# Sixty-four-row scores and state products widened to all 128 rows of the array in a hybrid-mixer trunk

## The chip, the cores and the metric

The kernel runs on one core of one Trainium2 chip. The metric is the device time of one execution in microseconds, from the first instruction to the last. Three executions of the kernel before stand beside one profiled execution.

## The reference

Two layers work on 256 context tokens and 256 latent tokens of width 1024. Each layer normalises, projects the input once, runs four mixers in parallel on the columns (A a gated recurrence, B an mLSTM, C grouped-query attention, D latent attention), merges them with gates, projects out, and adds a squared-ReLU MLP. Cut to what the change touches:

```python
# C: 8 query heads of 64 on 2 key heads; D: scores of 128 plain and 64 rotary columns
s = jnp.einsum('bqhgd,bmhd->bhgqm', qi, k) * scale
p = jax.nn.softmax(s, axis=-1)
return jnp.einsum('bhgqm,bmhd->bqhgd', p, v)
# B: q, k of 64 columns; cmat is the 64 x 128 state that the context left
s = jnp.einsum('bhtk,bhsk->bhts', qc, kc) * jnp.exp(dmat - m_t[..., None])
num = w_inter[..., None] * jnp.einsum('bhtk,bhkv->bhtv', qc, cmat) + jnp.einsum('bhts,bhsv->bhtv', s, vc)
```

In layer 0 the mixers answer for context and latent tokens, in layer 1 for the latent tokens alone.

## The kernel before, in words

Features or keys stand on the 128 partitions, so a product contracts over the rows of TensorE's array. Large products are made from numbers split into a high and a low part, in three passes (L193 to L195 and L215 to L217 for the input, gate, output and MLP weights, L164 to L166 for the branch weights). Weights come by DMA as `raw` tiles on SP's queue; ScalarE writes the high part `whi` (L136) and VectorE the low part `wlo` (L137).

The order of the work is written by hand: the string `ORDER` lists for each layer the steps of the mixers (`b` is one head of B on one side, `c` one pair of heads of C, `d` one head of D) and of the merges (`M0` to `M3`). A scheduler then lays the instructions of each engine out in one fixed order, in which the large products stand between the small ones of the mixers. Each engine takes its instructions in that order.

Scores of 64 columns (C, and the rotary part of D) are made by `score64`. `split_pair` puts a head's 64 high query rows on one half of the partitions and its low rows on the other half, in one tile `T`. `dup_key` writes the high key and the low key each on both halves. The first pass (L961) multiplies all 128 rows of `T` with the doubled high key. The second pass (L962) takes only the 64 high query rows and the 64 rows of the low key beside them. A softmax follows: maximum (L977, VectorE), exponential (L980, ScalarE), reciprocal and scaling (L982, L983, VectorE), and, two softmaxes later, the transposes of the probabilities on TensorE (L233), copied out by ScalarE (L989).

In B the scores of a head contract over 64 rows (L874). L879 broadcasts the running maximum with 100 rows. For each direction `d` the numerator sums up to three products into one PSUM tile (L907): probabilities `E` times values (128 rows, `bv` in the profile), and for the latents the scaled queries `qw` times the context state `C` (64 rows, those of the head). These are plain f32 operands, and each such product stands in the trace as two MATMULs. `qw` is written by ScalarE (L896) and VectorE (L897) on the head's 64 rows.

L400 is a product of the adaLN modulation that fills gaps, with 32 columns of the array. Scratch tiles of 2 KB a partition come from the pool `w2`, which has ten of them.

Of the kernel before, what the change touches and what calls it, by code (L numbers as in the profile page):

```python
# [23 lines left out]
# order of the mixers' steps and of the merges, by layer  # L24
# [16 lines left out]
class Trunk:  # L41
# [58 lines left out]
    def wide(self):  # L100
        """a pair of weight tiles out of the mixers' room."""
        t = self.t("w8", [128, 2, 1024], F32R)
        return t[:, 0, :], t[:, 1, :]

    def _prep(self):
        nc = self.nc
# [7 lines left out]
        n = 0  # L114
# [16 lines left out]
        with ExitStack() as st:  # L131
            # not in the way of a norm that the products wait for
            for ins in self.first[:2]:
                st.enter_context(self.tc.issue_after(ins))
            self.first = self.first[2:]
            nc.scalar.activation(out=hi[:, 0:n], in_=raw[:, 0:n], func=AF.Copy)  # L136
            nc.vector.tensor_tensor(out=lo[:, 0:n], in0=raw[:, 0:n], in1=hi[:, 0:n].bitcast(F32), op=ALU.subtract)  # L137
        self.ready[i] = (hi, lo)

    def get(self, key):  # L140
        if self.specs[self.next_use][2]:
            self.ada_sum()
        i = self.next_use
        assert self.specs[i][0] == key, (self.specs[i][0], key)
        # none ahead where a norm waits for the engines
        look = 0 if key[0] == "out" and key[2:] == (3, 1) or key[0] == "f2" and key[2:] == (3, 3, 1) else self.look
        while self.next_prep < min(i + 1 + look, len(self.specs)):
            self._prep()
        self.next_use += 1
        w = self.ready.pop(i)  # L150
        if self.specs[i][2]:
            # the modulation of a later phase, one chunk at a time
            n = self.next_use
            if n < len(self.specs) and self.specs[n][0][0] == "ada":
                self.ada_chunk(self.specs[n][0])
        return w

# [1 line left out]
    def mm3(self, out, pairs):  # L159
        """pairs: list of ((lhs_hi, lhs_lo), (rhs_hi, rhs_lo))."""  # L160
# [7 lines left out]
    def fm(self, W, t0, t1, nk=KT, c0=0, stride=128, act=None):  # L168
        """feature-major product: out[c, tok] for 128 columns of chunk W."""
# [7 lines left out]
    def fm2(self, key, t0, t1, act=None):  # L177
        """feature-major products for the 256 columns of two chunks, half of the rows in each."""
# [18 lines left out]
    def tm(self, key, i0):  # L197
        """token-major product: out[tok, 256 columns]; yields (first tile, psum [128, 2, 256])."""
# [9 lines left out]
    def tm_k(self, o, W, k, i):  # L208
# [4 lines left out]
        # one start per bank: it clears the written bits of both tiles  # L213
# [11 lines left out]
    def plan_cols(self, key, w, c0, halves=(0, 1), dest=None, fill=True):  # L225
        """256 columns of w, half of the rows at a time."""
# [9 lines left out]
    def setup(self):  # L236
# [22 lines left out]
        # puts a sum over the partitions in its row  # L259
# [13 lines left out]
        # conditioning columns  # L273
# [7 lines left out]
        # lower bounds of the second layer: softmax over the two layers  # L281
# [6 lines left out]
        # residual stream, feature-major; the first norm's statistics come from the token-major tiles  # L288
# [24 lines left out]
    def setup_late(self):  # L313
        """tables that only the mixers need."""
# [13 lines left out]
        # rotary tables with the key / query gains folded in  # L328
# [20 lines left out]
    def ada_vec(self, key):  # L349
        """the same on VectorE: running sums over the feature tiles, then one sum over the partitions."""  # L350
# [39 lines left out]
    def ada_chunk(self, key):  # L390
# [7 lines left out]
        for q in range(4):  # L398
            # one start per quadrant: it clears the written bits of both halves
# [33 lines left out]
    def stat(self, t0, k):  # L433
        """adds feature tile k of the tokens from t0 to the running sum of squares."""
# [25 lines left out]
    def warm_sqrt(self, src):  # L460
        """loads the square root's table ahead of its use."""
        d = self.sm([128, 1], "warm")
        self.nc.scalar.activation(out=d, in_=src, func=AF.Sqrt, scale=0.0)

    def rsqrt(self, ms, scale, out=None):
        """(scale * ms + eps) ** -0.5 on a small [128, n] operand."""
# [28 lines left out]
    # weights that follow the modulation of each feature tile  # L495
# [47 lines left out]
    def start(self):  # L543
        nc = self.nc
        W, out, at = {}, {}, {}
        for c in range(KT + 1):
# [7 lines left out]
            # the products, one feature tile behind  # L554
# [25 lines left out]
    def mixer_a(self, l, pre):  # L580
# [4 lines left out]
        if l:  # L585
            # the context first, while the latents are still being normalised
# [31 lines left out]
    def a_head(self, l, j, F, K, Q, KKs, q, V, O, q0, i0):  # L618
        nc = self.nc
        nt = 4 - i0  # L620
        # Q[0]: backward, Q[1]: forward
# [11 lines left out]
        for lev in range(8):  # L633
# [10 lines left out]
            else:  # L644
                # blocks of 128: across the two tiles of a side
# [8 lines left out]
            # grow the blocks  # L654
# [17 lines left out]
        # state left by the context  # L672
# [25 lines left out]
    def head_stats(self, O, out, i0):  # L698
        """mean squares of the heads of 128."""
# [6 lines left out]
    def readout(self, l, O, r, key, silu, gcol, i0, name):  # L706
        nc = self.nc
        for i in range(i0, 4):
            # half, for the gate is 1 + tanh
# [33 lines left out]
    def conv(self, l, qk, mt, ps, q0, scale):  # L743
        """three taps along the tokens of each side, then SiLU."""
# [15 lines left out]
    def mixer_b(self, l):  # L760
# [9 lines left out]
        for i2, ps in self.tm(("kv", l, 0), 0):  # L770
            # columns i_fwd, f_fwd, i_bwd, f_bwd to row groups 0, 64, 32, 96
# [8 lines left out]
        # log sigmoid of the forget gates on rows 0..3 (forward) and 32..35 (backward)  # L780
# [17 lines left out]
        # running maxima; the latents start from the maximum the context left  # L798
# [12 lines left out]
        # rows 64..: m = b + M  # L811
        nc.vector.tensor_tensor(out=UM[64:64 + R], in0=bc[0:R], in1=M[0:R], op=ALU.add)
        # -M as two parts on rows 0.. and 64.., for the broadcast over the partitions
# [4 lines left out]
        # broadcast of the end values over the partitions  # L818
# [7 lines left out]
        # u and m with tokens on partitions  # L826
# [10 lines left out]
        # keys, queries, values  # L837
# [8 lines left out]
        # context state  # L846
# [21 lines left out]
        for (sd, t0) in sides:  # L868
            for h in range(HEADS):
# [6 lines left out]
                for d in range(2):  # L876
# [5 lines left out]
                    full = d          # the key tile that meets both query tiles  # L882
# [11 lines left out]
                    if sd:  # L894
                        qw = self.t("w2", [128, 512])[:, 0:256]
                        nc.scalar.activation(out=qw[p0:p0 + 64], in_=pM[p0:p0 + 64, 0:256], func=AF.Exp, bias=ME[p0:p0 + 64, 1, row:row + 1])  # L896
                        nc.vector.tensor_tensor(out=qw[p0:p0 + 64], in0=qw[p0:p0 + 64], in1=qT[mt][p0:p0 + 64, t0:t0 + 256], op=ALU.mult)  # L897
                    pn = self.pm()
                    for tt in range(2):
# [4 lines left out]
                        if sd:  # L904
                            srcs.append((qw[p0:p0 + 64, tt * 128:(tt + 1) * 128], C[p0:p0 + 64, d, mt, :]))
# [16 lines left out]
    def rope(self, out, src, cos, sin, nh, eng):  # L922
        """out = src * cos + swap(src) * sin on [128, nh, 64]; cos, sin [128, 64]."""
# [10 lines left out]
    def dup_key(self, ps, p0, name):  # L934
        """hi and lo of the 64 rows of ps at p0, each on both halves of the partitions."""
# [10 lines left out]
    def split_pair(self, ps, q0, scale=1.0):  # L946
        """two heads of 64 rows: for each, hi on its own rows and lo on the other half."""
        nc = self.nc
        out = []
        for p0 in (0, 64):  # L950
# [5 lines left out]
            out.append((T, a))  # L956
        return out

    def score64(self, o, T, c, key, ns, start, stop):
        T, a = T  # L960
        self.nc.tensor.matmul(o, T[:, c], key[0][:, 0:ns], start=start, stop=False)  # L961
        self.nc.tensor.matmul(o, T[a, c], key[1][a, 0:ns], start=False, stop=stop)  # L962
# [10 lines left out]
    def softmax_t(self, ps, ns, PTdst):  # L973
        """softmax over the free axis of ps [128, ns]; probabilities transposed into PTdst [128, ns/128, 128]."""
# [19 lines left out]
    def run_later(self, depth=0):  # L994
        """second halves of the softmaxes, and what follows them, up to so many behind the first halves."""
# [114 lines left out]
    def mixer_d(self, l):  # L1110
# [11 lines left out]
        # latent keys and values  # L1122
# [11 lines left out]
        # rotary key, shared by the heads  # L1134
# [10 lines left out]
        # latent queries  # L1145
# [80 lines left out]
    def merge(self, l, r, Y, q0, js=range(4)):  # L1226
# [4 lines left out]
        for j in js:  # L1231
# [6 lines left out]
            if r == 3:  # L1238
                # the first weights of the MLP
# [66 lines left out]
    def ff(self, l, q0):  # L1306
        nc = self.nc
        # both halves of the hidden features in one tile where the latents alone need it
# [5 lines left out]
        for c in range(4):  # L1314
            if c == 0:
                # the context first, while the latents are still being normalised
# [17 lines left out]
            for p in range(4):  # L1334
                if l == 0 and c == 3 and p == 2:
                    self.ahead = [[self.get(("ai", 1, j, half)) for half in range(2)] for j in range(2)]
                if l == 0 and c == 3 and p == 3:
                    # the context first, so that its norm runs under the latents' products
# [33 lines left out]
    def run(self):  # L1372
# [81 lines left out]
        # final norm on the token-major output  # L1454
# [14 lines left out]
    def to_out(self, k):  # L1469
        """feature tile k of the latents, times the last gain, to the token-major output."""  # L1470
# [22 lines left out]
def layout(inputs):  # L1493
# [9 lines left out]
    # constants of the shapes  # L1503
# [32 lines left out]
```

## Time and profile before

| | |
|---|---|
| three executions | 1874.95, 1878.17 and 1880.63 us, median 1878.17 us |
| span of the profiled execution | 1878.2 us |
| TensorE busy | 1836.9 us (98% of the span), 11414 MATMULs |
| VectorE, ScalarE, GpSimd busy | 1135.8, 836.6 and 118.7 us |
| DMA | 235.26 MB, 125 GB/s on average |

The profiled execution is the span: nothing lies around it. In the timeline of TensorE the first number is the start in microseconds and the second the duration of the row; matmuls overlap, so what one occupies is the distance from its start to the next start, and not its duration. A form such as 64\*128 gives the rows and the columns of the array that the instruction uses.

### The profile page before, as it was taken

What the parts mean: (1) busy time and instruction counts of PE and PEld (TensorE: products, weight loads), DVE (VectorE), ACT (ScalarE), POOL (GpSimd) and SP (SyncE); (2) the same over time, 40 slices, a digit from 0 to 9 for tenths busy, and PEclk for the clock granted to TensorE, in tenths of its full rate; (3) what the DMA queues carried; (4) which work ended last, traced back from release to release, by engine and by line L of the source; (5) the groups of instructions that cost most, each with busy time, mean ns of one, the idle gap of its engine ahead of it and who ended that gap; (6) DMA issues with size and microseconds to landing.
All of it is one profiled execution on the core that took longest, in us unless ns stands there. A gap on an engine that the chain in (4) does not pass through costs nothing.

```text
span 1878.2 us, 28645 instructions
## 1 busy us (share of the span) xinstructions
PE 1836.9 (98%) x11414; PEld 1558.4 (83%) x11414; DVE 1135.8 (60%) x1983; ACT 836.6 (45%) x1487; POOL 118.7 (6%) x123
## 2 busy tenths in 40 slices
PE   7999999999999999999999999999999999999998
PEld 5788877799667778898777888988889969889998
DVE  5566654527654443566766665588574856575665
ACT  4343433434663333443333334344454664555555
POOL 0000000000001111111010000000000001101110
PEclk9999999999999999999999999999999999999999
DMA  9533353333112233314565665222334514454654
GB/s 284 178 91 108 117 147 123 90 107 90 46 34 68 68 124 101 113 46 146 168 190 177 185 187 158 79 68 68 89 114 141 161 52 135 144 161 145 185 185 136
DMA packets 222343, 235.26 MB, mean 125 GB/s; under 512 B 8320, under 2 KB 209408, under 8 KB 221952
## 3 DMA queue, kind: packets, MB, share of 16 engines
q1 hardware_dynamic: 222208, 233.42, 41.6%
q8 instruction: 90, 1.47, 0.3%
q14 instruction: 45, 0.37, 0.1%
HBM read 229.20 MB, written 4.19 MB: 124 GB/s over the span
## 4 chain that ended last, share of the span: by engine, by line
PE 86%; DVE 5%; DMA 4%; ACT 2%; issue 2%; SPq 0%; POOL 0%; ACTq 0%; DVEq 0%; POOLq 0%
PE pd L193 13%; PE pd L195 13%; PE pd L194 13%; PE pd L215 5%; PE pd L216 4%; PE pd L217 4%; PE pd L164 4%; PE pd L165 4%; PE pd L166 4%; DMA raw<-in_w_ada_dram 4%; PE pm L233 3%; PE pm L642 2%; DVE wlo L137 2%; PE pm L907 2%; PE pm L962 1%
## 5 line engine op out<-in xcount | busy, mean ns | idle before, releaser
L137 DVE TENSOR_TENSOR wlo<-raw,whi 128x1024 fp32r<-128x1024 f32 x305 | 385.9, 1265 | 301.4 <-ACT whi L136 299.8
L136 ACT ACTIVATE whi<-raw 128x1024 fp32r<-128x1024 f32 x305 | 322.0, 1057 | 402.6 <-PE pd L194 163.5
L195 PE MATMUL pd<-HH,wlo 128*128 128x256 f32 (+1 forms) x1104 | 373.2, 338 | 9.4 <-DVE wlo L137 9.4
L193 PE MATMUL pd<-HH,whi 128*128 128x256 f32 (+1 forms) x1104 | 374.0, 339 | 0.2 <-ACT whi L136 0.2
L194 PE MATMUL pd<-HL,whi 128*128 128x256 f32 (+1 forms) x1104 | 373.1, 338 | 0.0
L195 PEld LDWEIGHTS pd<-HH,wlo 128*128 128x128 f32 x1104 | 210.2, 190 | 34.5 <-DVE wlo L137 13.4
L193 PEld LDWEIGHTS pd<-HH,whi 128*128 128x128 f32 x1104 | 210.2, 190 | 25.5 <-issue 4.5
L194 PEld LDWEIGHTS pd<-HL,whi 128*128 128x128 f32 x1104 | 210.1, 190 | 22.8 <-issue 2.8
L195 PE MATMUL pd<-b,wlo 128*128 128x256 f32 (+1 forms) x528 | 175.7, 333 | 0.7 <-DVE wlo L137 0.6
L193 PE MATMUL pd<-b,whi 128*128 128x256 f32 (+1 forms) x528 | 175.8, 333 | 0.0
L194 PE MATMUL pd<-b,whi 128*128 128x256 f32 (+1 forms) x528 | 175.6, 333 | 0.0
L215 PE MATMUL pd<-whi,HH 128*128 128x256 f32 x592 | 169.3, 286 | 0.0
L217 PE MATMUL pd<-wlo,HH 128*128 128x256 f32 x592 | 168.9, 286 | 0.0
L216 PE MATMUL pd<-whi,HL 128*128 128x256 f32 x592 | 168.2, 284 | 0.0
L215 PEld LDWEIGHTS pd<-whi,HH 128*128 128x128 f32 x592 | 113.6, 192 | 4.2 <-issue 4.1
L216 PEld LDWEIGHTS pd<-whi,HL 128*128 128x128 f32 x592 | 113.6, 192 | 0.3 <-issue 0.2
L217 PEld LDWEIGHTS pd<-wlo,HH 128*128 128x128 f32 x592 | 113.5, 192 | 0.2 <-issue 0.2
L362 DVE SCALAR_TENSOR_TENSOR aacc<-raw,scol,aacc 128x1024 f32<-128x1024 f32 x56 | 73.0, 1310 | 64.6 <-DMA raw<-in_w_ada_dram 64.6
L195 PEld LDWEIGHTS pd<-b,wlo 128*128 128x128 f32 x528 | 100.4, 190 | 11.4 <-DVE wlo L137 2.2
L1248 POOL TENSOR_TENSOR mg<-mg,d 128x512 f32<-128x512 f32 (+1 forms) x48 | 54.9, 1147 | 870.7 <-DVE d L1247 590.7
L193 PEld LDWEIGHTS pd<-b,whi 128*128 128x128 f32 x528 | 100.4, 190 | 10.3 <-issue 0.8
L194 PEld LDWEIGHTS pd<-b,whi 128*128 128x128 f32 x528 | 100.4, 190 | 9.3
(418 smaller groups left out, 3319.9 us busy)
## 6 DMA issues: line engine op xcount, KB each, us to landing
raw<-in_w_in_dram SPq DMA_DIRECT2D x148, 512.0 KB, 3.8
raw<-in_w_ff_dram SPq DMA_DIRECT2D x128, 512.0 KB, 3.9
raw<-in_w_ada_dram SPq DMA_DIRECT2D x80, 512.0 KB, 4.1
raw<-in_w_branch_dram SPq DMA_DIRECT2D x24, 512.0 KB, 3.5
raw<-in_w_out_dram SPq DMA_DIRECT2D x16, 512.0 KB, 3.6
w<-in_w_ada_dram SPq DMA_DIRECT2D x28, 256.0 KB, 5.6
raw<-in_w_branch_dram SPq DMA_DIRECT2D x16, 256.0 KB, 3.9
spill<-X SPq DMA_DIRECT2D x1, 2048.0 KB, 8.2
```

What stands on the lines that cost most here:

```text
L136: nc.scalar.activation(out=hi[:, 0:n], in_=raw[:, 0:n], func=AF.Copy)
L137: nc.vector.tensor_tensor(out=lo[:, 0:n], in0=raw[:, 0:n], in1=hi[:, 0:n].bitcast(F32), op=ALU.subtract)
L164: nc.tensor.matmul(out, lh, rh, start=(i == 0), stop=False)
L165: nc.tensor.matmul(out, lh, rl, start=False, stop=False)
L166: nc.tensor.matmul(out, ll, rh, start=False, stop=(i == n - 1))
L193: nc.tensor.matmul(o, wh, act[0], start=(k == 0), stop=False, skip_group_check=True)
L194: nc.tensor.matmul(o, wh, act[1], start=False, stop=False, skip_group_check=True)
L195: nc.tensor.matmul(o, wl, act[0], start=False, stop=(k == KT - 1), skip_group_check=True)
L215: nc.tensor.matmul(o, hh, wh, start=first, stop=False, skip_group_check=True)
L216: nc.tensor.matmul(o, hl, wh, start=False, stop=False, skip_group_check=True)
L217: nc.tensor.matmul(o, hh, wl, start=False, stop=last, skip_group_check=True)
L362: nc.vector.scalar_tensor_tensor(out=acc, in0=raw, scalar=s, in1=acc, op0=ALU.mult, op1=ALU.add)
```

## The change

The second pass of `score64` contracts over all 128 rows: both query parts against the doubled low key, so that low times low is added to the score. The product with the context state contracts over all 128 rows too: the tile `qw` gets zeros on the 64 rows of the other head, by a memset on GpSimd, and the state of both heads is the other operand. The rest of the diff takes comments out.

```diff
@@ -892,7 +892,9 @@
                     if sd:
+
                         qw = self.t("w2", [128, 512])[:, 0:256]
+                        nc.gpsimd.memset(qw[64 - p0:128 - p0], 0.0)
                         nc.scalar.activation(out=qw[p0:p0 + 64], in_=pM[p0:p0 + 64, 0:256], func=AF.Exp, bias=ME[p0:p0 + 64, 1, row:row + 1])
...
@@ -902,7 +904,7 @@
                         if sd:
-                            srcs.append((qw[p0:p0 + 64, tt * 128:(tt + 1) * 128], C[p0:p0 + 64, d, mt, :]))
+                            srcs.append((qw[:, tt * 128:(tt + 1) * 128], C[:, d, mt, :]))
...
@@ -953,13 +955,13 @@
-            out.append((T, a))
+            out.append(T)
         return out
 
     def score64(self, o, T, c, key, ns, start, stop):
-        T, a = T
+
         self.nc.tensor.matmul(o, T[:, c], key[0][:, 0:ns], start=start, stop=False)
-        self.nc.tensor.matmul(o, T[a, c], key[1][a, 0:ns], start=False, stop=stop)
+        self.nc.tensor.matmul(o, T[:, c], key[1][:, 0:ns], start=False, stop=stop)
```

In the changed file the line numbers of these parts are two higher: L907 is L909 there, L962 is L964.

The order of the instructions on each engine stays as it was but for two places. On GpSimd the memsets join the queue. This is the queue in layer 0 between the setup of B and the first additions of the merge, of before (`nM` belongs to the setup of B, `mg` is the sum over the branches):

```order
L800 MEMSET w_205_2072 128x512
L815 MEMSET nM_2085 128x512
L1248 TENSOR_TENSOR mg_2659<-mg_2659,d_628_4909 128x512
```

and of the change, where eight memsets stand in between (and eight more at the same place of layer 1):

```order
L800 MEMSET w_205_2072 128x512
L815 MEMSET nM_2085 128x512
L897 MEMSET w_284_2861 64x256
L897 MEMSET w_288_2879 64x256
L897 MEMSET w_294_2909 64x256
L897 MEMSET w_298_2927 64x256
L897 MEMSET w_304_2957 64x256
L897 MEMSET w_308_2975 64x256
L897 MEMSET w_314_3005 64x256
L897 MEMSET w_318_3023 64x256
```

On TensorE one adaLN group moves at the last step of B in layer 0. Before, one of its four products (L400) stands ahead of the last products of B and three behind them:

```order
L195 MATMUL pd_3153<-HH,wlo_3159 128x512
L400 MATMUL pd_2172<-raw_3230,scol 32x256
L907 MATMUL pm_3019<-bv_2300,w_317_3010 128x129 x2
L907 MATMUL pm_3019<-C_2559,w_318_3016 128x129
L907 MATMUL pm_3019<-bv_2300,w_317_3010 128x129
L907 MATMUL pm_3019<-C_2559,w_318_3016 128x129
L400 MATMUL pd_2172<-raw_3230,scol 32x256 x3
```

With the change the four stand together:

```order
L195 MATMUL pd_3161<-HH,wlo_3167 128x512
L400 MATMUL pd_2172<-raw_3238,scol 32x256 x4
L164 MATMUL pd_3263<-ya_1891,whi_3202 128x512
L165 MATMUL pd_3263<-ya_1891,whi_3202 128x512
L909 MATMUL pm_3027<-bv_2300,w_317_3017 128x129 x2
L909 MATMUL pm_3027<-C_2559,w_318_3023 128x129
```

What does not move matters as well. At five of the sixteen steps of B on the latents the 64-row scores of the next head (L874) stand on TensorE beside the products with the state, before and after alike; this is such a step of before, from its first products with the values to the broadcast:

```order
L907 MATMUL pm_2881<-bv_2300,w_287_2872 128x129 x2
L874 MATMUL pm_2896<-w_225_2247,w_218_2156 128x256
L907 MATMUL pm_2881<-C_2559,w_288_2878 128x129
L907 MATMUL pm_2881<-bv_2300,w_287_2872 128x129
L907 MATMUL pm_2881<-C_2559,w_288_2878 128x129
L874 MATMUL pm_2896<-w_225_2247,w_218_2156 128x256
L879 MATMUL pm_2899<-nM_2085,rsel 128x256
```

In the change the same seven rows follow each other at this place, with L909 for L907; only the rows of the array that the two products with `C` use differ.

## Rows read from the trace of the kernel before

**Rows 1.** The page: busy time, share of the span and count of each engine.

```profile
PE 1836.9 (98%) x11414; PEld 1558.4 (83%) x11414; DVE 1135.8 (60%) x1983; ACT 836.6 (45%) x1487; POOL 118.7 (6%) x123
```

**Rows 2.** Timeline of TensorE, scores of D in layer 0: start, duration, instruction.

```profile
564.24 0.49 PE L962 MATMUL pm<-kr0l,w 64*128 64x512 f32 x1
564.66 0.50 PE L195 MATMUL pd<-HH,wlo 128*128 128x512 f32 x1
564.99 0.39 PE L193 MATMUL pd<-HH,whi 128*128 128x512 f32 x1
565.22 0.40 PE L194 MATMUL pd<-HL,whi 128*128 128x512 f32 x1
...
565.92 0.38 PE L233 MATMUL pm<-cst,p 128*128 128x128 f32 x2
566.05 0.47 PE L1191 MATMUL pm<-w,w 128*128 128x512 f32 x1
...
567.58 0.44 PE L233 MATMUL pm<-cst,p 128*128 128x128 f32 x2
567.77 0.48 PE L194 MATMUL pd<-HL,whi 128*128 128x512 f32 x1
```

**Rows 3.** Stretches, instructions of L962 alone: TensorE busy and count, weight loads likewise.

```profile
470.00:537.00 67.00, 13.70 (x32) 5.83 (x32) 1.00 0.11 32
1493.00:1533.00 40.00, 7.93 (x16) 2.92 (x16) 1.00 0.25 68
470.00:1616.00 1146.00, 32.98 (x72) 13.17 (x72) 1.00 0.38 114
```

**Rows 4.** Timeline of TensorE, a step of B in layer 0, forward direction.

```profile
334.65 0.39 PE L165 MATMUL pd<-ya,whi 128*128 128x512 f32 x1
334.98 0.49 PE L907 MATMUL pm<-C,w 64*128 64x129 f32 x2
335.39 0.71 PE L907 MATMUL pm<-bv,w 128*128 128x129 f32 x4
336.03 0.49 PE L907 MATMUL pm<-C,w 64*128 64x129 f32 x2
336.45 0.50 PE L166 MATMUL pd<-ya,wlo 128*128 128x512 f32 x1
336.79 0.40 PE L164 MATMUL pd<-ya,whi 128*128 128x512 f32 x1
```

**Rows 5.** Timeline of TensorE, the backward direction of the same step.

```profile
338.73 0.48 PE L874 MATMUL pm<-w,w 64*128 64x256 f32 x1
338.74 0.49 PE L907 MATMUL pm<-C,w 64*128 64x129 f32 x2
339.05 0.38 PE L874 MATMUL pm<-w,w 64*128 64x256 f32 x1
339.36 0.49 PE L907 MATMUL pm<-bv,w 128*128 128x129 f32 x2
```

**Rows 6.** Timeline of TensorE, the adaLN product ahead of B's last step in layer 0.

```profile
366.13 0.62 PE L400 MATMUL pd<-raw,scol 128*32 128x256 f32 x2
366.68 0.71 PE L907 MATMUL pm<-bv,w 128*128 128x129 f32 x4
```

**Rows 7.** The two stretches of mixer C: busy time of PE, PEld, DVE, ACT, POOL.

```profile
470.00:537.00 67.00, 66.78 (x325) 43.17 (x323) 44.90 (x107) 43.03 (x107) 2.75 (x2) 1.00 0.11 32
1493.00:1533.00 40.00, 40.00 (x237) 27.44 (x235) 30.72 (x67) 26.77 (x61) 4.03 (x4) 1.00 0.25 68
```

**Rows 8.** Timeline, mixer C in layer 0: a scaled softmax and its transposes.

```profile
497.89 0.34 DVE L983 TENSOR_SCALAR p<-p,srs 128x256 f32<-128x256 f32 x1
...
498.43 0.38 PE L233 MATMUL pm<-cst,p 128*128 128x128 f32 x2
```

**Rows 9.** GpSimd's groups by form: a memset of 512 columns.

```profile
L800 POOL MEMSET w<- 128x512 f32 x2 | 1.1, 525 | 3.0 <-PE pm L691 1.6 <-PE pm L690 1.3
```

## The prediction

> **What bounds the kernel now.** I read the page first: TensorE is busy for 1836.9 of 1878.2 us, VectorE for 60% and ScalarE for 45% [rows 1]. So a stretch ends earlier only if matmuls start closer together. A busy share of 98% hides how closely they stand, so I went to the timeline of TensorE and read distances from start to start. Two neighbouring passes with 512 columns on all 128 rows start 0.23 us apart (564.99 to 565.22) [rows 2]. That is the normal pace.
>
> Around a pass on 64 rows it is not kept. A 512-column matmul ahead of one holds 0.33 us (334.65 to 334.98) [rows 4], 0.10 over the pace. The 64-row pass with 512 columns holds 0.42 (564.24 to 564.66), 0.19 over. The first full-row pass behind it holds 0.33 (564.66 to 564.99), again 0.10 over [rows 2]. An excursion to 64 rows and back thus costs **0.39 us** beyond its own work. With transposes behind it the last part is smaller: a pair of them holds 0.19 (567.58 to 567.77) against 0.13 in the normal flow (565.92 to 566.05) [rows 2], so that excursion costs 0.35.
>
> **The change part by part.**
>
> *The second score pass.* There are 72 of them, 32 in C of layer 0, 16 in C of layer 1, the rest in D [rows 3]. Each stands alone between full-row passes (L961 ahead of it uses 128 rows), so each is a whole excursion. In the program's order 31 are followed by transposes and 41 by a matmul: 41 x 0.39 + 31 x 0.35 = 26.8 us. The widened pass should then keep the pace of L961, its twin in shape. The bounds: 72 x 0.29 = 20.9 if the surcharge on the follower stays for another reason, and 72 x 0.40 = 28.8 from the B rows below. I take 26.8, since all three parts were read at this very line.
>
> *The product with the state.* There are 32 of them, each two passes. In the forward step of [rows 4] two excursions lie between 334.65 and 336.79, 2.14 us. At the pace the same work is 0.23 for L165, 2 x 0.11 for each product with the state, 4 x 0.11 for the values (335.39 to 336.03 is 0.64, less a surcharge of 0.10 at either end, leaves 0.44 for four), and 0.23 for L166, together 1.34. The saving is 0.80, or 0.40 for each. Of the 32, 16 belong to forward steps and six to the three backward steps without L874 in their middle. One of these six has L874 right behind it; I set it to a loss of 0.1, since it shares its excursion now. So 21 x 0.40 - 0.1 = 8.3 us.
>
> The other ten stand in the five backward steps with L874 beside them, and there **the change loses**. Today L874 and the product with the state use different halves of the rows, and start 0.01 us apart (338.73 and 338.74); the whole group holds 0.63 us (338.73 to 339.36) [rows 5]. With the state on 128 rows they can't: L874's two passes need about 0.21 and 0.31 (the second as at 339.05 to 339.36, with the way out [rows 5]), then the state's first pass 0.21 and its second 0.11, together 0.84. That is 0.21 lost. In the second half of such a step the way out moves from the state to L874 and nothing is gained. So 5 x 0.21 = 1.05 us are lost, and this edit brings 8.3 - 1.05 = 7.2 us.
>
> *The adaLN product that joins its group.* One L400 product alone holds 0.55 us (366.13 to 366.68) [rows 6], most of it the way to 32 columns and back. Joined to the others it shares theirs: I take 0.5, between nothing and 0.55.
>
> *The memsets.* A memset of 512 columns takes 0.525 us on GpSimd [rows 9], so 256 columns should take about 0.26 as an estimate, 16 x 0.26 = 4.2 us in all. GpSimd is busy for 6% [rows 1], and in the order the memsets stand between B's setup and the merge's first additions, with nothing else there to hold up. The product with the state waits for its memset, and the first writer of a reused scratch tile sometimes does too. Ten tiles rotate, so a memset's tile has been free for some steps when B writes it. I put them at nothing; without that cover each costs 0.26 at the least.
>
> The sum on TensorE: 26.8 + 7.2 + 0.5 = **34.5 us**.
>
> **What is given back.** In C the softmaxes have to keep up. The stretch of layer 0 has 67 us with 44.9 on VectorE and 43.0 on ScalarE, that of layer 1 has 40 us with 30.7 and 26.8 [rows 7]. The scores there take 32 x 0.37 = 12 and 16 x 0.37 = 6 us out of TensorE, 55 and 34 remain, and VectorE would be busy for 82% and 90% of them. Between a score and its transposes two other scores stand, so TensorE arrives about 1.0 us earlier, while the chain of maximum, exponential and scaling keeps its length. Today the transposes start 0.20 us after the scaling has ended (497.89 + 0.34 = 498.23, then 498.43) [rows 8]. I went through the 48 rows of C in this way: in 27 the distance is under 1.0 us, and about 0.6 in the middle. So some 0.4 us is lacking in each of 27. If no two shared a stall that is 10.8 us; if the three that are under way at a time shared one, 3.6. I take 6, in between, and near the lower end, because VectorE's own waits for scores shrink as well. D has few softmaxes at once and long merges between them: nothing.
>
> 34.5 - 6 = 28.5 us, and 1878.2 - 28.5 = **1849.7 us**. The profiled execution took 1878.2 us, and the median of the runs is 1878.17, so nothing has to be carried over.
>
> **The rivals.**
>
> *All of it arrives.* If the softmaxes keep up, 1878.2 - 34.5 = 1843.7 us, and 1841 with the upper price of the scores. TensorE hardly waits for them now, which speaks for it; VectorE's 90% speaks against.
>
> *The softmaxes keep all that C gains.* If VectorE's queue becomes the pace of C in both layers, 18 of the 34.5 are lost: 1878.2 - 16.5 = 1861.7 us. For it speaks the 0.20 us of [rows 8]; against it that VectorE would still have 10 us free in layer 0 [rows 7].
>
> *The rows don't matter.* If a 64-row pass was dear for another reason (its operands, or the accumulation into the same PSUM tile), scores and state products save nothing, the five steps lose 1.05 and the adaLN product brings 0.5: 1878.7 us. Against it: the surcharge stands at L962 and at L907 alike, with other operands, and on full-row passes behind them [rows 2, 4]. The Trainium skill's page "TensorE: Matmul & The Clock Gate" speaks for this rival in Part 3, "Packing small matmuls": a matmul over few rows takes as long as one over 128, what row tiles bring is that they run at once, and a weight load overlaps a running matmul only where the row groups differ. By that rule the change gains nothing and gives up an overlap, as this rival has it. The trace agrees on the overlap (L874 and the state product 0.01 us apart [rows 5]) and disagrees on the price of a lone 64-row pass, 0.42 us where 0.23 is the pace [rows 2].
>
> *Slower: the state product waits for GpSimd.* The memset is the first to touch a reused tile, so it waits for the tile's last readers, and GpSimd takes its queue in order: one late release holds the next memsets too, and TensorE stops at the product, with the merge's matmuls behind it. At 1.8 us for each of the 16 the gain of 28.5 is gone; at 2.5 us, 40 us in all, the time is 1889.7. Against it stand GpSimd's 6% [rows 1] and ten rotating tiles.
>
> **How the numbers follow.** A measurement of this kernel tells a change of about 0.3% (5.6 us) from none. Chances: the forecast with part of C given back, 1844 to 1857 us, 0.68; all of it arrives, below 1844, 0.12; C keeps its gain, 1857 to 1866, 0.12; the rows don't matter, 0.04; slower by GpSimd, 0.03, or by something unseen, 0.01. The range from 1841 to 1862 leaves out the outer parts of the second and third, and the last three, under 2 in 10. Faster by over 0.3%: 0.68 + 0.12 + 0.12, and 0.01 for a part of the GpSimd case, 0.93. The same: 0.04. Slower: 0.03.
>
> **What the profile after should show.** L964 on 128 rows, and 0.23 us for 512 columns at L961, at L964 and at the matmul behind it. Two state passes and four value passes in a forward step 0.11 apart. L874 and the state product one after the other, with the group of 0.63 at 0.84. The stretch of C in layer 0 near 59 us and that of layer 1 near 36, with waits of TensorE for L985 (now L983) where none were. I am wrong if the distances around L964 stay at 0.33 and 0.42, if TensorE waits for a memset, or if C keeps its 67 us at the normal pace.

## The result, and the profile after

The change takes 1851.32 us (median of four executions, 1845.39 to 1856.88), the kernel before beside it 1878.72 us (1874.95 to 1880.63, four). The ratio is 0.9865, with a 95% interval of 0.985 to 0.988: faster by 27.4 us. The forecast was 1849.7 us. The profiled execution of the change has a span of 1850.2 us and took 1851.94.

The page of the change, busy time by engine (PE is TensorE, PEld its weight loads, DVE VectorE, ACT ScalarE, POOL GpSimd):

```profile
PE 1805.8 (98%) x11414; PEld 1554.8 (84%) x11414; DVE 1134.1 (61%) x1983; ACT 836.3 (45%) x1487; POOL 123.1 (7%) x139
```

TensorE runs the same 11414 matmuls in 31.1 us less busy time [rows 1], the span is 28.0 us shorter. The page alone doesn't say where; the timeline does. Scores of D in layer 0, after, to be read from start to start:

```profile
549.99 0.40 PE L963 MATMUL pm<-kr0h,w 128*128 128x512 f32 x1
550.22 0.39 PE L964 MATMUL pm<-kr0l,w 128*128 128x512 f32 x1
550.45 0.40 PE L195 MATMUL pd<-HH,wlo 128*128 128x512 f32 x1
550.68 0.39 PE L193 MATMUL pd<-HH,whi 128*128 128x512 f32 x1
```

The second pass and its neighbours now stand 0.23 us apart each, where the 64-row pass held 0.42 and its follower 0.33 [rows 2]. The first pass reaches this pace only in the flow of the large products: 512 columns of L963 that stand right behind transposes hold 0.31 to 0.34 us after, and 0.40 to 0.41 before. The stretches of C after (start and end, length, busy time of PE, PEld, DVE, ACT, POOL; the last three numbers are the granted clock of TensorE as a share of full speed, the share of DMA and its GB/s), and below them L964 alone from C to the end of D in layer 1 (PE and PEld):

```profile
465.10:524.20 59.10, 57.79 (x325) 41.09 (x324) 44.63 (x107) 42.90 (x108) 2.75 (x2) 1.00 0.12 37
1472.00:1507.20 35.20, 35.13 (x236) 27.59 (x234) 30.08 (x66) 26.31 (x61) 5.07 (x4) 1.00 0.25 77
...
465.10:1590.00 1124.90, 25.56 (x72) 13.64 (x72) 1.00 0.38 116
```

C of layer 0 went from 67.0 to 59.1 us, C of layer 1 from 40.0 to 35.2 (its stretch of before had one matmul more), and the 72 second passes from 32.98 us busy to 25.56 [rows 3, 7]. But in layer 0 TensorE is idle for 59.10 - 57.79 = 1.31 us, against 67.00 - 66.78 = 0.22 before.

B's step in layer 0, forward direction, and then the backward direction with L874 in it, after:

```profile
333.72 0.40 PE L165 MATMUL pd<-ya,whi 128*128 128x512 f32 x1
333.95 0.38 PE L909 MATMUL pm<-C,w 128*128 128x129 f32 x2
334.17 0.61 PE L909 MATMUL pm<-bv,w 128*128 128x129 f32 x4
...
335.07 0.39 PE L164 MATMUL pd<-ya,whi 128*128 128x512 f32 x1
...
336.46 0.61 PE L909 MATMUL pm<-bv,w 128*128 128x129 f32 x4
337.00 0.70 PE L874 MATMUL pm<-w,w 64*128 64x256 f32 x2
337.63 0.49 PE L909 MATMUL pm<-C,w 128*128 128x129 f32 x2
337.95 0.39 PE L909 MATMUL pm<-bv,w 128*128 128x129 f32 x2
338.18 0.39 PE L909 MATMUL pm<-C,w 128*128 128x129 f32 x2
338.49 0.70 PE L874 MATMUL pm<-w,w 64*128 64x256 f32 x2
339.12 0.38 PE L879 MATMUL pm<-nM,rsel 100*128 100x256 f32 x1
339.34 0.39 PE L164 MATMUL pd<-ya,whi 128*128 128x512 f32 x1
```

The forward step holds 1.35 us (333.72 to 335.07), 2.14 before [rows 4]. The backward step became longer: its first group holds 0.95 us (337.00 to 337.95) instead of 0.63 [rows 5]. The adaLN group at B's last step, all of it in one place now:

```profile
362.63 0.64 PE L400 MATMUL pd<-raw,scol 128*32 128x256 f32 x8
363.20 0.50 PE L164 MATMUL pd<-ya,whi 128*128 128x512 f32 x1
```

Eight passes hold 0.57 us, about as much as two held before [rows 6]. GpSimd's group of memsets:

```profile
L897 POOL MEMSET w<- 64x256 f32 x16 | 4.9, 306 | 253.9 <-ACT bden L913 112.4 <-DVE ssq L704 70.2 <-PE pm L909 62.5
```

**Where the 28.0 us came from.** I matched TensorE's instructions of both traces one by one and compared every distance from a start to the next. In the table "C and D" are measured between the same two large matmuls on either side (455.2 and 708.0 us of before in layer 0, 1468.3 and 1620.1 in layer 1), B between 285.1 and 375.2 and between 1380.1 and 1424.3. The same marks serve for all kernels below, each against the profiled execution of before.

| us against before | up to B | B, layer 0 | C and D, layer 0 | MLP and layer 1 up to B | B, layer 1 | C and D, layer 1 | rest |
|---|---|---|---|---|---|---|---|
| the change | -0.9 | -4.0 | -12.35 | -1.3 | -2.7 | -7.2 | +0.3 |

Within C and D the distances at the 72 second passes and their two neighbours fell by 25.4 us (16.8 in C, 8.6 in D). All other distances there grew by 5.9 us: 3.9 in C, 2.0 in D (4.3 in layer 0, 1.6 in layer 1). That is what was given back. B's 6.7 us are 5.6 of the state products, 0.5 of adaLN, and 0.5 of three places at the first value passes of a step (L907 at 363.01, 1395.37 and 1415.96 of before), where a wait of TensorE got shorter by 0.22, 0.13 and 0.19.

One large growth, in the timeline of C in layer 0 after (all engines; the bracket is idle time and its releaser):

```profile
480.17 1.29 POOL L1250 TENSOR_TENSOR mg<-mg,d 128x512 f32<-128x512 f32 x1 [125.94 <-DVE srs L984]
...
480.49 1.26 DVE L985 TENSOR_SCALAR p<-p,srs 128x512 f32<-128x512 f32 x1
...
480.87 0.40 PE L166 MATMUL pd<-yb,wlo 128*128 128x512 f32 x1
...
481.85 0.35 DVE L985 TENSOR_SCALAR p<-p,srs 128x256 f32<-128x256 f32 x1
481.89 0.63 PE L233 MATMUL pm<-cst,p 128*128 128x128 f32 x4 [0.62 <-DVE srs L984]
```

TensorE has finished with L166 and stands for 0.62 us until the reciprocal and scaling are there; from L166 to the transposes are 1.02 us, where before they were 0.46. The scaling of these four transposes is the one of 480.49. It took 1.26 us, where the middle of all 72 is 0.48, and it lies beside an addition on GpSimd.

The lateness can be counted. In C of layer 0, 6 of the 32 groups of transposes started within 0.25 us of the end of their scaling before; in the change it is 15. In C of layer 1 it was 1 of 16 and is now 6.

### The profile page after: what moved, and what is told of

The parts are those of the page before. It is cut to its first block, busy times and chain, and to the rows that moved or that the text cites. A ratio compares the mean times of both kernels' runs of the same rounds, so it can differ in the third digit from the quotient of the medians.

```text
span 1850.2 us, 28703 instructions
## 1 busy us (share of the span) xinstructions
PE 1805.8 (98%) x11414; PEld 1554.8 (84%) x11414; DVE 1134.1 (61%) x1983; ACT 836.3 (45%) x1487; POOL 123.1 (7%) x139
## 4 chain that ended last, share of the span: by engine, by line
PE 81%; DVE 7%; DMA 6%; ACT 3%; issue 2%; SPq 0%; POOL 0%; ACTq 0%; DVEq 0%; POOLq 0%
PE pd L193 12%; PE pd L195 12%; PE pd L194 12%; DMA raw<-in_w_ada_dram 5%; PE pd L215 5%; PE pd L216 4%; PE pd L217 4%; PE pd L164 4%; PE pd L165 4%; PE pd L166 4%; PE pm L642 2%; PE pm L233 2%; DVE wlo L137 2%; PE pm L909 1%; PE pm L1100 1%
## 5 line engine op out<-in xcount | busy, mean ns | idle before, releaser
L437 ACT ACTIVATE w<-X 128x256 f32<-128x256 f32 x120 | 48.1, 413 | 128.9 <-DVE X L1257 128.9
```

## The experiments

Three questions: are the surcharges around a 64-row pass, and nothing else, what the change removes; what are the 5.9 us that came back; and is the loss in B's backward steps due to the 64-row scores that are left? The stretches of all of them:

| us against before | up to B | B, layer 0 | C and D, layer 0 | MLP and layer 1 up to B | B, layer 1 | C and D, layer 1 | rest |
|---|---|---|---|---|---|---|---|
| e1_scores_only | -0.3 | -0.1 | -12.95 | -0.4 | 0.0 | -7.2 | +3.0 |
| e2_state_only | -0.3 | -4.0 | +0.5 | -0.5 | -2.7 | +0.2 | 0.0 |
| e3_rows96 | -0.4 | -4.0 | -12.2 | +1.3 | -2.7 | -7.2 | -0.3 |
| e4_other_weights | -0.4 | -3.9 | -12.4 | -0.8 | -2.7 | -7.1 | -0.3 |
| e5_short_after | -1.0 | -4.0 | -12.4 | -1.6 | -2.7 | -7.0 | -0.5 |
| e6_short_before | -0.9 | -0.1 | +0.5 | 0.0 | 0.0 | +0.3 | -0.2 |
| e7_b_scores128 | +0.3 | -7.4 | -12.45 | -0.9 | -5.1 | -7.2 | -0.8 |
| e8_memsets4 | +1.0 | -3.9 | -12.5 | -0.1 | -2.7 | -7.1 | -0.4 |

Stretches that an edit doesn't touch differ by up to 0.1 us in B and 0.6 in C and D, by up to 1.6 in the others, and once by 3.0 (the rest of e1_scores_only, spread over the products behind D of layer 1; its cause was not looked for). I take that as the scatter of one profiled execution.

**The scores alone**, on top of the kernel before:

```diff
-        self.nc.tensor.matmul(o, T[a, c], key[1][a, 0:ns], start=False, stop=stop)
+        self.nc.tensor.matmul(o, T[:, c], key[1][:, 0:ns], start=False, stop=stop)
```

> Only the second score pass goes to 128 rows; the product with the state stays on 64 rows, and no memset is added. Theory (each lone excursion to 64 rows costs 0.35 to 0.39 us on TensorE, and the softmaxes give a part back): in the trace of the change the distances around L964 lost 25.4 us and other distances in C and D grew by 5.9, so 19.5 us are saved, 1859 us, ratio 0.990. Rival (the state product and the memsets brought the larger part, for example by another order): 1870 us or more, ratio 0.996 or more.

Measured: 1861.70 us beside 1882.37 for the kernel before, ratio 0.9887 (0.9868 to 0.9907). C and D gain in both layers what they gain in the change, B nothing.

**The state product alone:**

```diff
+                        nc.gpsimd.memset(qw[64 - p0:128 - p0], 0.0)
...
-                            srcs.append((qw[p0:p0 + 64, tt * 128:(tt + 1) * 128], C[p0:p0 + 64, d, mt, :]))
+                            srcs.append((qw[:, tt * 128:(tt + 1) * 128], C[:, d, mt, :]))
```

> Only the product with the state goes to 128 rows, with its sixteen memsets; the second score pass stays on 64 rows. Theory: the trace of the change has 6.7 us less in the two stretches of B, so 1872 us, ratio 0.9965; the group of L874 with the state product in a backward step takes 0.84 us where it took 0.63. Rival (the product waits for GpSimd's memset): 1878 us or more, and a wait of TensorE for GpSimd in the rows.

Measured: 1873.38 us, ratio 0.9952 (0.9933 to 0.9971) against the same runs of before. Both layers' B gain 6.7 us as in the change, the adaLN group that moves included, and C and D nothing. The group of L874 with the state product holds 0.95 us as in the change, not the 0.84 of the expectation. TensorE waits for GpSimd nowhere in the trace. So the two halves of the change add, and neither needs the other.

**The second pass on 96 rows**, from the change:

```diff
-        self.nc.tensor.matmul(o, T[:, c], key[1][:, 0:ns], start=False, stop=stop)
+        self.nc.tensor.matmul(o, T[0:96, c], key[1][0:96, 0:ns], start=False, stop=stop)
```

> The change, but the second score pass contracts over the rows 0 to 95 alone, in place of all 128; the scores are then not those of the reference. Theory (what costs is leaving the form in which the whole array is one block, and 96 rows do not leave it): 1851 us, ratio 0.9865, and 0.23 us for 512 columns around L964. Rival (any count of rows other than that of the neighbours costs): the 19.5 us come back, 1871 us, with 0.33, 0.42 and 0.33 around L964.

Measured: 1853.75 us, ratio 0.9848 (0.9827 to 0.9869), stretches as in the change. Its timeline at the place of D shown above:

```profile
550.55 0.40 PE L963 MATMUL pm<-kr0h,w 128*128 128x512 f32 x1
550.79 0.39 PE L964 MATMUL pm<-kr0l,w 96*128 96x512 f32 x1
551.02 0.39 PE L195 MATMUL pd<-HH,wlo 128*128 128x512 f32 x1
```

The form is 96\*128, and the pace is 0.23 us throughout. A row count below 128 is not what costs; 64 rows are.

**Other stationary columns in the second pass**, from the change:

```diff
-        self.nc.tensor.matmul(o, T[:, c], key[1][:, 0:ns], start=False, stop=stop)
+        o2 = c.start + 128 if c.start % 256 == 0 else c.start - 128
+        self.nc.tensor.matmul(o, T[:, o2:o2 + 128], key[1][:, 0:ns], start=False, stop=stop)
```

> The change, but the second score pass takes the 128 query columns of the other token tile, so that it no longer loads the same stationary operand as the first pass; the scores are then not those of the reference. Theory (form of the array): no difference from the change, 1851 us, ratio 0.9865. Rival (the gain comes from two passes in a row with the same weights): up to 72 x 0.1 to 0.3 us come back, 1858 to 1871 us.

Measured: 1853.20 us, ratio 0.9842 (0.9821 to 0.9862), stretches as in the change. That both passes now load the same stationary operand (the weights that stay in the array) brings nothing; this theory fell.

**A shorter scaling**, in the change and, as a control, in the kernel before (the probabilities beyond the first 32 columns stay unscaled):

```diff
-        nc.vector.tensor_scalar(out=P, in0=P, scalar1=r, scalar2=None, op0=ALU.mult)
+        nc.vector.tensor_scalar(out=P[:, 0:32], in0=P[:, 0:32], scalar1=r, scalar2=None, op0=ALU.mult)
```

> The change, but VectorE scales only the first 32 of each softmax's 256 or 512 columns, so that the chain between a score and its transposes is about 0.3 to 0.4 us shorter and VectorE has about 25 us less to do; the probabilities are then not normalised. Together with the next kernel, which has the same shortening without the change. Theory (in C and D the faster scores run into the softmax chain, 5.9 us are given back there): most of it comes back, 4 us, so 1847 us, and the gap to its partner is 32 us where the change alone brought 28. Rival (what is given back goes to something else, PSUM tiles or the weights): no difference from the change beyond that of the partner, gap 28 us or less.

> The kernel before with the same shortening: only 32 columns of each softmax are scaled, the probabilities are then not normalised. Theory: TensorE does not wait for the softmaxes before the change, so nothing is gained, ratio 1.000, 0.998 at the least. Rival (the chain was already the pace of C): ratio 0.997 or less.

Measured: 1853.12 us, ratio 0.9858 (0.9841 to 0.9875), and the control 1879.95 us, 1.0005 (0.9994 to 1.0016). The change with it gains no more than without. VectorE's groups by form, of this kernel first and then of the change:

```profile
L985 DVE TENSOR_SCALAR p<-p,srs 128x32 f32<-128x32 f32 x72 | 17.9, 250 | 3.1
```

```profile
L985 DVE TENSOR_SCALAR p<-p,srs 128x512 f32<-128x512 f32 x48 | 24.6, 514 | 1.8
```

A sixteenth of the columns still takes 250 ns, so the chain became at most 0.26 us shorter, and the order of the small products on TensorE moved too. The expectation was missed, and the run doesn't decide what came back; another remedy was needed.

**B's scores on 128 rows as well** (L874), with copies of the queries whose other half is zero, from the change:

```diff
+                qz = self.t("p2", [128, 512])[:, 0:256]
+                nc.gpsimd.memset(qz[64 - p0:128 - p0], 0.0)
+                nc.gpsimd.tensor_copy(qz[p0:p0 + 64], qT[mt][p0:p0 + 64, t0:t0 + 256])
...
-                    nc.tensor.matmul(pS[:, st * 256:(st + 1) * 256], kT[mt][p0:p0 + 64, t0 + st * 128:t0 + (st + 1) * 128],
-                                     qT[mt][p0:p0 + 64, t0:t0 + 256], start=True, stop=True, skip_group_check=True)
+                    nc.tensor.matmul(pS[:, st * 256:(st + 1) * 256], kT[mt][:, t0 + st * 128:t0 + (st + 1) * 128],
+                                     qz, start=True, stop=True, skip_group_check=True)
```

> The change, and the last 64-row products too: the scores of B contract over 128 rows, with zero-filled copies of the queries made on GpSimd (a memset and a copy for each head and side, in a tile of the pool that the softmaxes use later). Theory (form of the array): seven groups of four passes save 0.39 and three times 0.09 us, five split groups twice 0.39 and 0.09 and the 0.21 that the change lost there: 4.6 + 4.8 us, 1842 us, ratio to the kernel before 0.981. Rival (the copies on GpSimd are late, or the 64-row passes of two halves ran at once and lose that): no gain on the change, 1851 us or more.

Measured: 1846.72 us (1846.02 to 1847.98), ratio 0.9826 (0.9809 to 0.9842). B gains 12.5 us against before, 5.8 beyond the change: the direction held, the size was short of the expectation (9.4). It answers the third question: the five backward steps with L874, 0.44 to 0.50 us longer than before in the change, are 0.27 to 0.34 shorter than before here. The backward step in its timeline:

```profile
335.92 0.61 PE L912 MATMUL pm<-bv,w 128*128 128x129 f32 x4
336.36 0.60 PE L877 MATMUL pm<-p,w 128*128 128x256 f32 x2
336.79 0.39 PE L912 MATMUL pm<-C,w 128*128 128x129 f32 x2
...
338.02 0.40 PE L164 MATMUL pd<-ya,whi 128*128 128x512 f32 x1
```

From the four value passes to L164 it holds 2.10 us, in the change 2.88 (336.46 to 339.34). A pair of L877 holds 0.43, so a 256-column pass of these operands takes about 0.21 at full rows too; part of what looked like surcharge at L874 was its own work. That is where the expectation was too high: of the seven groups of L874 that stand alone six brought 0.39 to 0.40 us and one 0.19, where 0.66 was expected.

**Four times the memsets**, from the change:

```diff
-                        nc.gpsimd.memset(qw[64 - p0:128 - p0], 0.0)
+                        for _ in range(4):
+                            nc.gpsimd.memset(qw[64 - p0:128 - p0], 0.0)
```

> The change with every memset of the query tile made four times over. Theory (GpSimd's work stands beside everything else): 1851 us as the change, ratio 0.9865, at most 1 us more. Rival (the product waits for GpSimd): 48 more memsets of 0.27 us, up to 13 us more, 1864 us.

Measured: 1853.89 us, ratio 0.9862 (0.9844 to 0.9880), stretches as in the change. GpSimd's group of this kernel:

```profile
L898 POOL MEMSET w<- 64x256 f32 x64 | 19.5, 306 | 242.9 <-ACT bden L914 113.9 <-DVE ssq L704 69.9 <-PE pm L910 43.1
```

14.6 us more on GpSimd leave B as it was: the memsets are hidden.

**Transposes three softmaxes behind their scores instead of two**, in the change and, as a control, in the kernel before:

```diff
-        self.bufs = {"w2": 10, "d2": 3, "p2": 2, "w4": 4, "w8": 4, "b16": 3}
+        self.bufs = {"w2": 12, "d2": 3, "p2": 2, "w4": 4, "w8": 4, "b16": 3}
...
-        self.depth = 2
+        self.depth = 3
...
-        P = self.t("p2", [128, 512])[:, 0:ns]
+        P = self.t("w2", [128, 512])[:, 0:ns]
```

> The change, with the transposes three softmaxes behind their scores instead of two (probabilities in the scratch pool, which gets two tiles more, 12). Theory (TensorE waits for softmaxes that come too late in C and D, 3.8 and 2.0 us given back): most of it returns, span of C in layer 0 and 1 together 3 us shorter than in the change, D 1 us, time near 1847 us. Rival (what is given back is scatter, or the VectorE queue itself is the pace, which a longer lag does not shorten): 1851 to 1853 us. A third: the new order of the small products costs of its own, over 1853 us.

> The kernel before with the same lag of three and the same pools, as a control. Theory: before hardly waits for softmaxes, so that nothing returns, within 1.5 us of the kernel before. Rival (the longer lag is worth something, or costs something, by its order alone): as many us off the kernel before as e9_depth3 is off the change.

Measured: 1848.57 us, ratio 0.9839 (0.9822 to 0.9855), and the control 1879.78 us, 0.9997 (0.9987 to 1.0007). The times point the expected way, but the interval overlaps that of the change. The stretches say more: C and D of layer 0 stand at -14.8 us (the change -12.35), in the control at +0.5. The order in layer 1 moves past the last mark, so there I measure up to 1640.3 us: -8.8, where the change has -7.8, and -0.9 in the control. Thus the longer lag returns 2.4 us in layer 0, where it brings the kernel before nothing, and in layer 1 no more than it brings the kernel before. C and D of layer 0, stretch of TensorE (length, busy), for before, the change, the longer lag, and its control:

```profile
455.20:708.00 252.80, 251.25 (x1178) 1.00 0.23 67
```

```profile
450.40:690.80 240.40, 237.20 (x1178) 1.00 0.23 71
```

```profile
451.90:689.90 238.00, 235.80 (x1177) 1.00 0.24 71
```

```profile
454.70:707.90 253.20, 251.46 (x1179) 1.00 0.23 67
```

Idle time is 1.55 us before, 3.20 in the change, 2.20 with the longer lag and 1.74 in the control. TensorE's waits in the same stretch (total, times, longest), of the change and then of the longer lag:

```profile
PE pm L1194 <- DVE w L971: 1.4, 3, 0.9
PE pm L233 <- DVE srs L984: 0.6, 1, 0.6
PE pm L233 <- DVE p L985: 0.5, 3, 0.2
PE pm L963 <- DVE w L956: 0.2, 1, 0.2
```

```profile
PE pm L1194 <- DVE w L971: 1.4, 3, 0.9
PE pm L233 <- DVE w L956: 0.6, 1, 0.6
```

The waits of the transposes for reciprocal and scaling are gone; the one for the high and low parts of D's queries (L971) stands, and one for `split_pair` (L956) grew from 0.2 to 0.6. These named waits make up only 0.7 of the 2.4 us, and idle time 1.0: a matmul's row runs past the start of the next, so a longer distance doesn't always show as idle. The lateness says it more plainly. With the longer lag 6 of the 32 groups of transposes in C of layer 0 start within 0.25 us of their scaling, as before, and not the 15 of the change.

**Both together**, B's scores on 128 rows (the copies in the scratch pool) and the lag of three:

```diff
+                qz = self.t("w2", [128, 512])[:, 0:256]
...
-        self.depth = 2
+        self.depth = 3
```

The rest of the diff is as in the two kernels above. A first form, e11_b128_depth3, kept the copies in `p2` beside the twelve tiles; these don't fit on a partition together, so it has no time.

> The change with B's scores on 128 rows (as in e7_b_scores128, whose copies of the queries now lie in the scratch pool) and the lag of three softmaxes together. By the stages the lag of three brings 3.3 us to the change and 1.3 to the kernel before, and the scores of B 3.2 to the change. If both stand apart, the gains add: 1851.3 - 3.2 - 3.3 = 1844.8 us, spans of B as in e7_b_scores128 and of C and D as in e9_depth3. Rival (they share the scratch pool, and one takes what the other gains): 1847 to 1849 us.

Measured: 1846.60 us (1842.34 to 1848.81), ratio 0.9828 (0.9813 to 0.9844). In the trace the gains add: span 1842.2 us, against 1844.7 of e7_b_scores128 and 1848.3 of e9_depth3; B -7.4 and -5.0, C and D of layer 0 -14.85. The times don't tell it from e7_b_scores128, whose ratio is 0.9826. Both are below the change and the kernel before; which of them is the better one stays open.

## Why the prediction was right, and where its terms were off

**The mechanism held.** The surcharge on the 64-row pass went away at all 72 L964, those ahead of it and behind it at most of them, and the forward step of B holds 1.35 us where 1.34 was worked out. The rival that rows don't matter fell with e1_scores_only and e2_state_only. It rested on the Trainium skill's "TensorE: Matmul & The Clock Gate", Part 3 and the table under "Why this matters for your kernels". Another page of the skill, "TensorEngine Tiling (Array Packing)", says under "Key Properties" that a change of the tiling mode drains TensorE, without a price. The rows agree, and here the price is 0.10 + 0.19 + 0.10 us for a way to 64 rows and back, while 96 rows cost nothing. That it is a drain was not shown; that the cost lies with the 64-row form was.

The weight loads of TensorE show one thing more. These are the loads of the second pass and of its follower at the place in D, before and after:

```profile
564.23 0.18 PEld L962 LDWEIGHTS pm<-kr0l,w 64*128 64x128 f32 x1 [0.36 <-issue]
564.65 0.19 PEld L195 LDWEIGHTS pd<-HH,wlo 128*128 128x128 f32 x1 [0.24 <-issue]
```

```profile
549.99 0.19 PEld L964 LDWEIGHTS pm<-kr0l,w 128*128 128x128 f32 x1
550.23 0.19 PEld L195 LDWEIGHTS pd<-HH,wlo 128*128 128x128 f32 x1
```

After, the load of L964 starts with the pass ahead of it (549.99) and lies under that pass. Before, it started only with its own pass (564.24), and the follower's load with the follower (564.66). So it was at all 72, within 4 ns; with 96 rows the load stands ahead again, by 0.23 us in the middle, as in the change. Two loads that are not hidden, 0.18 + 0.19 us, would be 0.37 of the 0.39 us. That is an estimate from these rows, and no run separated the loads from the rest.

**The scores: 26.8 forecast, 25.4 measured.** The part ahead of the pass is 0.091 us in the middle of the 72 rather than 0.10, which makes 0.6 us. In some places another cause holds the same distance: ahead of eight passes it shrank by less than 0.04 us, and behind one pass of C in layer 0 the follower holds 0.47 us instead of 0.34, though its surcharge is gone.

**The state products: 7.2 forecast, 5.6 measured.** The main step that failed is the five backward steps with L874 in their middle. The forecast had the first group at 0.84 us; it holds 0.95. Its term for the pair of L874 was 0.21 + 0.31 us; the pair holds 0.63 (337.00 to 337.63), since the way to 64 rows ahead of it and the one back are now paid around a pair that shares nothing. And "in the second half ... nothing is gained" was too kind. These are rows of before from that half, with the start of [rows 5] behind them:

```profile
339.78 0.37 PE L907 MATMUL pm<-C,w 64*128 64x129 f32 x1
339.78 0.48 PE L874 MATMUL pm<-w,w 64*128 64x256 f32 x1
...
340.41 0.38 PE L879 MATMUL pm<-nM,rsel 100*128 100x256 f32 x1
```

The two halves of the array overlapped here too (339.78 twice). The value passes ahead went from 0.42 to 0.23 us, the rest from 0.63 (339.78 to 340.41) to 0.94 (338.18 to 339.12): 0.12 lost. The step lost 0.32 + 0.12 = 0.44 us instead of 0.21, and the five together 2.3 us instead of 1.05. That is 1.2 us of the 1.6 that are lacking. The other 0.4 are shared by the eight forward steps, 6.2 us where 6.4 was worked out, and the three backward steps without L874 in their middle, 1.7 instead of 1.9. The 0.5 us of the three shorter waits at value passes was in no term.

**AdaLN: 0.5 forecast, 0.5 measured** (the distances at the split group fell by 0.54). **The memsets: nothing forecast, nothing measured** (e8_memsets4); a memset of 256 columns on 64 partitions takes 0.31 us, not 0.26.

**Given back: 6 in C and nothing in D forecast; 3.9 and 2.0 measured.** The sum is right by luck, for the place was not. That D with "few softmaxes at once" gives nothing back is the step that failed: the same late products, the low part of D's queries (L971, one distance from 0.15 to 0.55 us) and the scaling (0.23 to 0.55 us at 551.37), end distances there. The trace of before had the sign: read as C was read, three of D's 16 groups of transposes in layer 0 stood less than 1.0 us behind their scaling, the nearest 0.15 us. In C the forecast of 6 lay above what came, 3.9, which is close to its lower bound of 3.6. That these are softmaxes that come too late is shown for layer 0: with a longer lag the waits for L984 and L985 vanish and 2.4 of its 4.3 us return, and not so in the kernel before. For the 1.6 us of layer 1 the releasers of single waits say the same, and so does the count of late transposes in its C (1 of 16 before, 6 after), but the longer lag returned nothing of its own, so that part is argued and not shown.

**Outside the change 1.9 us fell away** (before B, in the MLP, at the end). Other kernels differ there by -1.6 to +3.0 us in a stretch, the control e10_before_depth3 by -0.8 in the MLP, so I take this as scatter.

**The step from span to time.** The span came within 0.5 us of the 1849.7 forecast. Part of that is luck: the stretches that the change touches gave 25.4 + 6.7 - 5.9 = 26.2 us where 28.5 was forecast, and the 1.9 us from elsewhere made up most of the rest. (The lowest case of the rivals is 1841.7 by its own terms, not 1841.) In the profiled execution of before, time and span are equal; in the change 1.7 us lie around the span, and 1.7 to 2.1 in all the others. So "nothing has to be carried over" held for that one execution only.

## What to carry to other kernels

Read TensorE from start to start and price a pass on fewer rows with both its neighbours: a lone 64-row pass between full ones was dear, and rows of zeros or of harmless extra terms removed it. Widen all passes of a group together: where one 64-row pass is left beside the widened ones, it loses the partner with which it shared the way and the array. When TensorE gains in a stretch with a chain through other engines, expect part of the gain back, or give that chain a longer lag: here it returned 2.4 of 4.3 us in one stretch and nothing of its own in another.

## What the runs showed of the hardware

- The 96-row form keeps the full pace (0.23 us for 512 columns beside 128-row passes), the 64-row form does not (0.42).
- Around the 64-row pass the weight loads of 0.18 and 0.19 us start with their own passes (within 4 ns at all 72); where the second pass has 96 or 128 rows its load starts 0.23 us ahead in the middle, under the pass before.
- A VectorE scaling of 512 columns took 1.26 us beside a GpSimd addition of 1.29 us; the middle of 72 is 0.48. It started 0.32 us behind the addition and ended 0.29 us after it (481.75 and 481.46). All three scalings of the change that took over 0.65 us lie beside such an addition, and so do the two of before (0.90 and 0.69). In these traces who starts first decides: these five started 0.32 to 1.12 us behind an addition, and each ended 0.28 or 0.29 us after its end; the six that started 0.16 us ahead of one kept 0.48 us. The Trainium skill's "SBUF — State Buffer", "Who interferes with whom", has GpSimd and VectorE in its two-port modes share a pair of ports, which the one that starts first holds for a whole instruction while the other stands. The trace agrees in kind, but a scaling that stood until the addition's end would have ended 0.48 us after it, and not 0.28 or 0.29. No run here took the addition away. A faster TensorE changes which scalings and additions meet.
- A scaling of 32 columns takes 0.25 us, one of 512 columns 0.51 on average: shortening the operand doesn't shorten the chain in proportion.
